# Expert products computed ahead: whole fp32 rows in full-width products, and a later gather in the second layer

## The chip, the cores and the metric

The kernel runs on one core of one Trainium2 chip. The metric is device time in microseconds (us), lower is better. Before the change the median of 3 runs is 5698.48 us (5694.15 to 5700.12).

## The reference

The model is a trunk of two layers over 128 context tokens and 512 latent tokens of width 1024. Each layer has a token mixer (gated linear attention, a short convolution, windowed attention) and then a feed-forward part with 16384 experts, in which each token uses 8 x 16 = 128 of them. The change lies in that second part:

```
q = (xf @ w_pq).reshape(nt, 8, 2, 128)
s = einsum('thpc,hpkc->thpk', q, keys)          # scores against 2 x 128 keys
s1, i1 = top_k(s[:, :, 0], 16);  s2, i2 = top_k(s[:, :, 1], 16)
top_s, top_pos = top_k(s1[..., None] + s2[..., None, :], 16)   # 16 of 256 pairs
eidx = i1 * 128 + i2 at top_pos;  gate = softmax(top_s)
act = gelu(einsum('td,thkd->thk', x, u_tab[eidx]))
out = einsum('thk,thkd->td', gate * act, v_tab[eidx])
```

An expert is a row of `u_tab` and a row of `v_tab`, both of width 1024.

## The kernel before

**Two ways to compute the experts.** For the context tokens and for the first 128 latent tokens of each layer, the rows that a token needs are gathered by indirect DMA (`peer_gather`): per token tile 128 rows of u and 128 rows of v, each fetch 128 x 4 KB, issued by POOL (L915) into one of the slots `grow`. DVE reduces a u row with the token's h (L920), or adds a weighted v row to `gacc` (L932). For the other 384 latent tokens (`TD`) all 16384 experts are computed densely, 128 tiles of 128 experts: S = u tile x h (contraction over 1024 = 8 blocks), GELU, times a gate map G that holds the gate of each (expert, token) and is zero elsewhere, and then the product with the v tile into six accumulators.

**Split products.** A dense product is made of three products: each fp32 operand is split into H (rounded to fp32r, by ACT) and L (the rest, by DVE or POOL), and `mm3` adds H x H, H x L and L x H. For an expert tile `u_hidden` loads 512 KB (`uraw`), ACT makes `uH` (L1012), DVE makes `uL` (L1014), and TensorE runs 8 x 3 products with 384 columns (L196 to L198). hH and hL of the tokens are there already.

**Stages of a layer's second half.** (1) Scores: `routing_keys`, after the mixer. In the first layer the second layer's context pass is run here too. (2) `routing_pairs` for the four token tiles (DVE: top 16 of the pairs); in the first layer this is done in stage 1, in the second one here. (3) Gate maps: `gate_map` for token tiles 1 to 3, each 4 chunks of 4 steps. In a step DVE, POOL and ACT build one-hot rows `oa` and `ob` of 8 tokens, TensorE multiplies them (two groups of 4, `pa` and `po`), and ACT and DVE copy the results into `stage`; after 4 steps the 2 MB of `stage` (one buffer) are stored to `gdr` in DRAM. (4) The dense stage `peer_dense`, 64 pairs of expert tiles.

**Work computed ahead.** In stages 1 to 3, `u_ahead` computes S for the first `AHEAD` = (108, 64) expert tiles, copies it from its bank (tag `po`, two banks, shared with the `po` group of a gate step) to `ust` and stores it to `sdr`. The dense stage takes first the pairs that were not computed ahead (u product, then v product: part one, 32 pairs in the second layer) and then those that were (it loads S from `sdr`, only the v product: part two, 32 pairs).

**What sets the order.** `u_ahead` and `peer_gather` are background generators. `tick` (L152) advances each by its rate for every step of the foreground work: `RU` is the rate of the tiles ahead, `RG` = (2.0, 1.056) that of the gather in stages 2 and 3; in the dense stage the gather's rate is set so that its remaining steps spread evenly over it (`e[1]`, L1396). The scheduler then puts each engine's instructions into one fixed order, in which the engine runs them. A tile's slots are reused in turn: `uraw` has `ucfg["n"]` slots (2 in the gate maps), and the load of the next but one tile waits until a slot's last reader is done.

Of the kernel before, what the change touches and what calls it, by code (L numbers as in the profile page):

```python
# [43 lines left out]
def kernel(ctx: ExitStack, tc: tile.TileContext, A: dict, O: list):  # L44
# [23 lines left out]
    def po2(shape, name="po"):  # L68
        return psum.tile(shape, F32, tag="po", name=name, bufs=2)
# [937 lines left out]
    def u_hidden(l, e, hH, hL):  # L1007

        raw = ucfg["p"].tile([128, 8, 128], F32, name="uraw", bufs=ucfg["n"])
        nc.sync.dma_start(raw.rearrange("p k c -> p (k c)"), A["u_T"][l, e])  # L1010
        uH, uL = t4k([128, 8, 128], "uH", F32R), t4k([128, 8, 128], "uL", F32R)
        act(uH, raw, AF.Copy)  # L1012
        m = 8 - ucfg["pool_l"]
        V.tensor_sub(uL[:, :m, :], raw[:, :m, :], uH[:, :m, :].bitcast(F32))  # L1014
        if m < 8:
            nc.gpsimd.tensor_sub(uL[:, m:, :], raw[:, m:, :], uH[:, m:, :].bitcast(F32))
        ahead = e < AHEAD[l]
        S = po2([128, TD]) if ahead else pb([128, TD])
        if not ahead:
            tick()  # L1020
        for k in range(8):
            mm3(S, uH[:, k, :], uL[:, k, :], hH[:, k, 128:], hL[:, k, 128:], k == 0, k == 7)
        return S

    def u_ahead(l, hH, hL):

# [10 lines left out]
    def peer_dense(s, l, hH, hL, dp, e_g, gout, gp):  # L1037
# [40 lines left out]
                    then(t)  # L1078

        for n, i in enumerate(pairs):  # L1080
            up(i)
            if n and n < 63:
                down()
                down()
# [171 lines left out]
    PIN = (1, 0, 1)  # L1256
    PU = (0, 0, 0, 3)
    OB = ('APDAPADA', 'APDAPADA')
    RG = (2.0, 1.056)
    RU = ((0.7, 1.0), (0.84, 0.8))  # L1260

    CONV = (1, 0.12, (0, 2), (4.8, 4.0), 0.7, 0.2)
# [69 lines left out]
    for l in range(DEPTH):  # L1332
        with pool("g_ctx") as gp:
            gcfg.update(p=gp, tag="grow", n=5, m=0)
            with w_pool(2, 2, PL[1]):
                if l:
                    lat.open_cv()
                    run(lat.finish(l))
                    e = bg_add(peer_gather(C, l, 0, ro_c[0], ro_c[1], gp, after=lat.end), RATE[l][0], PR[2])
                    mixer_lat(l, e, range(4))  # L1340
                else:
                    first = First(gp)
                    e = bg_add(first.work(), RATE[0][0], PR[2])
                    mixer_lat(l, e, range(CONV[0], 4), first)
            bg_drain(e)
        if l + 1 == DEPTH:
            with pool("ln_out") as lp:
                run(ln_finish(C, 2 * DEPTH, ln_rows(lp, 4)))
            nc.gpsimd.dma_start(y_prompt[0], C.x[0])
        with pool("e_lat") as ep:  # L1350
            hH, hL = lat.h
            vals, idxs = route_bufs(Lt, ep)
            ro = {}
            more = l + 1 < DEPTH

            def front(qp):
                yield from routing_keys(Lt, l, hH, hL, vals, idxs, qp)
                if more:
                    for t in range(4):
                        yield from routing_pairs(t, vals, idxs, ep, qp, ro)  # L1360

            ahead = pool("u_t6")
            ucfg.update(p=ahead.__enter__(), n=1, pool_l=PU[0])
            eu = bg_add(u_ahead(l, hH, hL), RU[l][0], PR[0])
            with w_pool(3, 2, PL[2]), pool("ro_lat", 2) as qp:
                with pool("ln_lat2") as lp:
                    run(ln_finish(Lt, 2 * l + 1, ln_rows(lp, 4), True))
                e = bg_add(front(qp), BG[4], PR[5])
                if more:
                    ro_c = ctx_front(l + 1, ec)  # L1370
                bg_drain(e)
            ahead.__exit__(None, None, None)
            gout = []
            ucfg["l"] = l
            with pool("g_lat") as gp, pool("u_lat") as up_:
                ucfg.update(p=up_, n=2, pool_l=PU[1 + l])
                with pool("gm") as qp:
                    gcfg.update(p=qp, tag="grow", n=5, m=1)

                    def pairs(t):  # L1380
                        if not more:
                            for _ in routing_pairs(t, vals, idxs, ep, qp, ro):
                                tick()
                    eu[1] = RU[l][1]
                    pairs(0)
                    e = bg_add(peer_gather(Lt, l, 0, ro[0][0], ro[0][1], gp, gout), RG[l], PR[1])
                    pairs(1)
                    for t in range(1, 4):
                        if t < 3:
                            pairs(t + 1)  # L1390
                        gate_map(t, ro[t], qp)
                    bg_drain(eu)
                ucfg["pool_l"] = PU[3]
                with pool("dense") as dp, w_pool(8, 3, PL[3 + l]):
                    gcfg.update(p=wcfg["p"], tag="wraw", n=8, m=2)
                    e[1] = (256 + LAG - e[3]) / (256 - AHEAD[l] - 10)  # L1396
                    peer_dense(Lt, l, hH, hL, dp, e, gout, gp)


# [109 lines left out]
```

## Time and profile before

| | |
|---|---|
| median of 3 runs (range) | 5698.48 us (5694.15 to 5700.12) |
| the profiled execution: its own time / span of the profile | 5700.02 / 5698.2 us |
| TensorE busy / DVE / ACT / POOL | 90% / 75% / 36% / 44% |
| first layer, gate maps | 2141 to 2505 us |
| second layer, routing pairs and 24 tiles ahead | 4370 to 4506 us |
| second layer, gate maps and 40 tiles ahead | 4506 to 4835 us |
| second layer, dense stage, part one / part two | 4867 to 5356 / 5356 to 5660 us |

The shares over the whole span mix stages with different limits, so the stages of the table are read one by one. A matmul's busy time in the rows is longer than the time for which it holds the array: successive matmuls overlap, so the price of one is the distance between the starts of two. TensorE's granted clock is a mean over a stretch; at each moment it is at one of two levels, 2.4 or 1.2 GHz (1.0 and 0.5).

### The profile page before, as it was taken

How to read it: one execution, taken by the hardware profiler on the slowest of the kernel's cores; microseconds unless marked ns; L12 is line 12 of the kernel's file. 1: busy time of each engine (PE TensorE's matmuls, PEld its weight loads, DVE VectorE, ACT ScalarE, POOL GpSimd, SP SyncE). 2: the span in 40 equal slices, each digit the busy share in tenths (PEclk: the TensorE clock that was granted, in tenths of full speed). 3: DMA queues.
4: the chain of work that ended last, by engine and by line, in shares of the span. 5: the costliest groups of instructions: out<-in, count | busy, mean ns of one | idle time of the engine just before them, and what ended most of it. 6: DMA issues, size and time to landing. Idle time of an engine off the chain costs nothing. (4 is left out here: it accounts for less than half of the span.)

```text
span 5698.2 us, 78492 instructions
## 1 busy us (share of the span) xinstructions
PE 5144.1 (90%) x28598; PEld 4475.9 (79%) x28598; DVE 4257.4 (75%) x7555; ACT 2052.4 (36%) x3456; POOL 2493.1 (44%) x1907
## 2 busy tenths in 40 slices
PE   8998899888899998899999788999989788899997
PEld 6887778767788998888777677777778788799876
DVE  3328878878554868887777798888879998677667
ACT  2214434221232226653333344332223457333332
POOL 1112434676210007876555533456750466444332
PEclk9999999999899999999999899999989899999999
DMA  7762457887666667899999533678842776888895
GB/s 293 269 240 94 156 176 231 297 293 259 212 213 237 226 229 269 307 338 323 325 309 325 186 132 123 225 258 294 293 158 101 233 266 246 310 273 271 285 320 198
DMA packets 456708, 1395.09 MB, mean 245 GB/s; under 512 B 42880, under 2 KB 184832, under 8 KB 413312
## 3 DMA queue, kind: packets, MB, share of 16 engines
q1 hardware_dynamic: 303248, 833.73, 41.3%
q0 software_dynamic: 153072, 556.34, 28.7%
q8 instruction: 225, 3.69, 0.3%
q14 instruction: 163, 1.34, 0.1%
HBM read 1275.29 MB, written 114.62 MB: 244 GB/s over the span
## 5 line engine op out<-in xcount | busy, mean ns | idle before, releaser
L915 POOL DMA_INDIRECT grow<-in_peer_u_dram,eidx x512 | 689.1, 1346 | 675.8 <-DVE gjunk L920 235.8
L915 POOL DMA_INDIRECT grow<-in_peer_v_dram,eidx x512 | 669.3, 1307 | 630.2 <-DVE gacc L932 282.5
L932 DVE SCALAR_TENSOR_TENSOR gacc<-grow,gw,gacc 128x1024 f32<-128x1024 f32 x508 | 707.1, 1392 | 94.8 <-DMA grow<-in_peer_v_dram,eidx 89.8
L176 POOL TENSOR_TENSOR wl<-wraw,wh 128x640 fp32r<-128x640 f32 (+1 forms) x260 | 417.0, 1606 | 703.0 <-ACT wh L172 646.9
L920 DVE SCALAR_TENSOR_TENSOR gjunk<-grow,gh 128x1024 bf16<-128x1024 f32 x512 | 678.1, 1324 | 60.8 <-DMA grow<-in_peer_u_dram,eidx 56.6
L172 ACT ACTIVATE wh<-wraw 128x1024 fp32r<-128x1024 f32 (+1 forms) x388 | 515.2, 1342 | 522.8 <-PE pa L197 207.4
L174 DVE TENSOR_TENSOR wl<-wraw,wh 128x1408 fp32r<-128x1408 f32 (+2 forms) x388 | 555.5, 1434 | 177.2 <-ACT wh L172 177.0
L196 PE MATMUL acc<-wh,daH 128*128 128x512 f32 x1536 | 610.9, 398 | 60.3 <-ACT daH L110 43.8
L198 PE MATMUL acc<-wh,daL 128*128 128x512 f32 x1536 | 612.7, 399 | 14.6 <-DVE daL L111 14.3
L197 PE MATMUL acc<-wl,daH 128*128 128x512 f32 x1536 | 608.4, 396 | 0.5 <-DVE wl L174 0.5
L196 PE MATMUL pa<-hH,wh 128*128 128x512 f32 x1312 | 544.0, 415 | 48.0 <-DVE th L742 12.3
L198 PE MATMUL pa<-hH,wl 128*128 128x512 f32 x1312 | 536.5, 410 | 7.2 <-DVE wl L174 7.2
L197 PE MATMUL pa<-hL,wh 128*128 128x512 f32 x1312 | 536.8, 409 | 0.5 <-DVE hL L111 0.4
L196 PE MATMUL po<-hH,uH 128*128 128x384 f32 x1376 | 490.5, 356 | 26.6 <-ACT uH L1012 10.6
L198 PE MATMUL po<-hH,uL 128*128 128x384 f32 x1376 | 476.6, 347 | 18.4 <-DVE uL L1014 18.1
L197 PE MATMUL po<-hL,uH 128*128 128x384 f32 x1376 | 474.5, 345 | 0.0
L1012 ACT ACTIVATE uH<-uraw 128x1024 fp32r<-128x1024 f32 x256 | 270.8, 1058 | 563.3 <-PE po L197 192.7
L196 PEld LDWEIGHTS acc<-wh,daH 128*128 128x128 f32 x1536 | 294.2, 192 | 130.6 <-ACT daH L110 55.3
L1014 DVE TENSOR_TENSOR uL<-uraw,uH 128x1024 fp32r<-128x1024 f32 (+1 forms) x256 | 285.4, 1115 | 120.0 <-ACT uH L1012 120.0
L985 POOL TENSOR_SCALAR ob<-iota,tt,tt 128x128 f32<-128x128 f32 x192 | 299.3, 1564 | 172.6 <-ACT tt L966 91.8
L198 PEld LDWEIGHTS acc<-wh,daL 128*128 128x128 f32 x1536 | 294.2, 192 | 94.3 <-DVE daL L111 33.4
L196 PEld LDWEIGHTS pa<-hH,wh 128*128 128x128 f32 x1312 | 255.3, 195 | 115.6 <-DVE th L742 14.3
(365 smaller groups left out, 11788.5 us busy)
## 6 DMA issues: line engine op xcount, KB each, us to landing
wraw<-in_w_in_dram SPq DMA_DIRECT2D x168, 1024.0 KB, 5.7
uraw<-in_u_T_dram SPq DMA_DIRECT2D x256, 512.0 KB, 4.7
wraw<-in_v_n_dram SPq DMA_DIRECT2D x256, 512.0 KB, 6.1
wraw<-in_w_mod_dram SPq DMA_DIRECT2D x48, 1024.0 KB, 6.0
wraw<-in_w_branch_dram SPq DMA_DIRECT2D x48, 1024.0 KB, 5.6
gdr<-stage SPq DMA_DIRECT2D x24, 2048.0 KB, 10.4
G<-gdr SPq DMA_DIRECT2D x64, 768.0 KB, 8.0
sdr<-ust SPq DMA_DIRECT2D x172, 192.0 KB, 4.4
```

What stands on the lines that cost most here:

```text
L172: act(H, raw, AF.Copy)
L174: V.tensor_sub(L[:, :m], raw[:, :m], H[:, :m].bitcast(F32))
L176: nc.gpsimd.tensor_sub(L[:, m:], raw[:, m:], H[:, m:].bitcast(F32))
L196: nc.tensor.matmul(out, aH, bH, start=start, stop=False)
L197: nc.tensor.matmul(out, aH, bL, start=False, stop=False)
L198: nc.tensor.matmul(out, aL, bH, start=False, stop=stop)
L915: nc.gpsimd.indirect_dma_start(out=g, out_offset=None, in_=A[tab + str(l)], in_offset=bass.IndirectOffsetOnAxis(ap=eidx[:, j:j + 1], axis=0))
L920: pin(V.scalar_tensor_tensor(junk, g, 1.0, h, op0=OP.mult, op1=OP.mult, accum_out=w[:, j:j + 1]))
L932: pin(V.scalar_tensor_tensor(acc, g, w[:, j:j + 1], acc, op0=OP.mult, op1=OP.add))
L985: (nc.gpsimd if w == "P" else V).tensor_scalar(ob[:, k, :], iota128, TT[1][:, j:j + 1], TT[2][:, j:j + 1], op0=OP.is_equal, op1=OP.mult)
L1012: act(uH, raw, AF.Copy)
L1014: V.tensor_sub(uL[:, :m, :], raw[:, :m, :], uH[:, :m, :].bitcast(F32))
```

## The change

For some of the tiles ahead, TensorE multiplies the loaded rows as they are. `whole_h` adds hH and hL back together into `hF` (one DVE addition of 128 x 3072), and `u_hidden` then does 8 full fp32 products `uraw` x `hF` and no split. This holds for the tiles in the gate maps of the first layer (48 of 108) and for all 64 of the second layer; there `whole_h` runs twice, once in each pool. The dense stage's own tiles stay split. In the second layer the gather's rate in stages 2 and 3 falls from 1.056 to 0.4, and in the dense stage it is 1.35 in part one and what is left, spread evenly, in part two. Counted in the program order on DVE, the 256 gathered rows of the second layer stand as follows: before its first dense pair 83 before and 32 now (20 and 30 of them ahead of the first gate step), in part one 119 and 168, in part two 54 and 56.

```diff
--- before.py
+++ after.py
@@ -1008,6 +1008,12 @@
 
         raw = ucfg["p"].tile([128, 8, 128], F32, name="uraw", bufs=ucfg["n"])
         nc.sync.dma_start(raw.rearrange("p k c -> p (k c)"), A["u_T"][l, e])
+        hF = ucfg.get("hF")
+        if hF is not None:
+            S = po2([128, TD])
+            for k in range(8):
+                nc.tensor.matmul(S, raw[:, k, :], hF[:, k, :], start=k == 0, stop=k == 7)
+            return S
         uH, uL = t4k([128, 8, 128], "uH", F32R), t4k([128, 8, 128], "uL", F32R)
         act(uH, raw, AF.Copy)
         m = 8 - ucfg["pool_l"]
@@ -1021,6 +1027,12 @@
         for k in range(8):
             mm3(S, uH[:, k, :], uL[:, k, :], hH[:, k, 128:], hL[:, k, 128:], k == 0, k == 7)
         return S
+
+    def whole_h(hH, hL, p):
+
+        hF = p.tile([128, 8, TD], F32, name="hF", bufs=1)
+        V.tensor_add(hF, hH[:, :, 128:].bitcast(F32), hL[:, :, 128:].bitcast(F32))
+        return hF
 
     def u_ahead(l, hH, hL):
 
@@ -1078,6 +1090,8 @@
                     then(t)
 
         for n, i in enumerate(pairs):
+            if not i and RD[l]:
+                e_g[1] = (256 + LAG - e_g[3]) / (AHEAD[l] - 10)
             up(i)
             if n and n < 63:
                 down()
@@ -1256,7 +1270,8 @@
     PIN = (1, 0, 1)
     PU = (0, 0, 0, 3)
     OB = ('APDAPADA', 'APDAPADA')
-    RG = (2.0, 1.056)
+    RG = (2.0, 0.4)
+    RD = (None, 1.35)
     RU = ((0.7, 1.0), (0.84, 0.8))
 
     CONV = (1, 0.12, (0, 2), (4.8, 4.0), 0.7, 0.2)
@@ -1360,7 +1375,8 @@
                         yield from routing_pairs(t, vals, idxs, ep, qp, ro)
 
             ahead = pool("u_t6")
-            ucfg.update(p=ahead.__enter__(), n=1, pool_l=PU[0])
+            up_ = ahead.__enter__()
+            ucfg.update(p=up_, n=1 if more else 2, pool_l=PU[0], hF=None if more else whole_h(hH, hL, up_))
             eu = bg_add(u_ahead(l, hH, hL), RU[l][0], PR[0])
             with w_pool(3, 2, PL[2]), pool("ro_lat", 2) as qp:
                 with pool("ln_lat2") as lp:
@@ -1376,6 +1392,7 @@
                 ucfg.update(p=up_, n=2, pool_l=PU[1 + l])
                 with pool("gm") as qp:
                     gcfg.update(p=qp, tag="grow", n=5, m=1)
+                    ucfg["hF"] = whole_h(hH, hL, qp)
 
                     def pairs(t):
                         if not more:
@@ -1390,10 +1407,10 @@
                             pairs(t + 1)
                         gate_map(t, ro[t], qp)
                     bg_drain(eu)
-                ucfg["pool_l"] = PU[3]
+                ucfg.update(pool_l=PU[3], hF=None)
                 with pool("dense") as dp, w_pool(8, 3, PL[3 + l]):
                     gcfg.update(p=wcfg["p"], tag="wraw", n=8, m=2)
-                    e[1] = (256 + LAG - e[3]) / (256 - AHEAD[l] - 10)
+                    e[1] = RD[l] or (256 + LAG - e[3]) / (256 - AHEAD[l] - 10)
                     peer_dense(Lt, l, hH, hL, dp, e, gout, gp)
 
 
```

TensorE in the second layer's gate maps, before: two gate steps and the first three of 24 products of one tile between them (`uH`, `uL` are the halves of the u tile, `oa`, `ob` the one-hot rows).

```order
L993 MATMUL pa<-oa,ob 128x128 x4
L993 MATMUL po<-oa,ob 128x128 x4
L196 MATMUL po<-hH,uH 128x384
L197 MATMUL po<-hL,uH 128x384
L198 MATMUL po<-hH,uL 128x384
...
L993 MATMUL pa<-oa,ob 128x128 x4
L993 MATMUL po<-oa,ob 128x128 x4
```

The same place in the changed kernel.

```order
L993 MATMUL pa<-oa,ob 128x128 x4
L993 MATMUL po<-oa,ob 128x128 x4
L993 MATMUL pa<-oa,ob 128x128
L1015 MATMUL po<-hF,uraw 128x384 x8
L993 MATMUL pa<-oa,ob 128x128 x3
L993 MATMUL po<-oa,ob 128x128 x4
L1015 MATMUL po<-hF,uraw 128x384 x8
```

The tiles stand between the same steps as before; a tile is 8 products in place of 24.

DVE in the same stage, before (`gjunk` is a gathered u row, `ust` the copy of S).

```order
L1014 TENSOR_TENSOR uL<-uraw,uH 128x1024
L980 TENSOR_TENSOR oa<-iota_87,tt_37444 128x1024
L985 TENSOR_SCALAR ob<-iota_87,tt_37448,tt_37452 128x128 x2
L920 SCALAR_TENSOR_TENSOR gjunk,gw<-grow,gh 128x1024
L1031 COPY ust<-po 128x384
L1014 TENSOR_TENSOR uL<-uraw,uH 128x1024
L997 COPY stage<-po 128x4x128
```

And changed.

```order
L997 COPY stage<-po 128x4x128
L980 TENSOR_TENSOR oa<-iota_87,tt_35518 128x1024
L985 TENSOR_SCALAR ob<-iota_87,tt_35522,tt_35526 128x128 x2
L1043 COPY ust<-po 128x384
L997 COPY stage<-po 128x4x128
```

The split and the gathered row are gone from between the gate step's own instructions.

The DMA queue of SP around one store of `stage` in the second layer, before, with the semaphores that each issue waits for.

```order
L1001 DMA gdr<-stage 128x4096 [waits DMAHW3_49,DVE_49,Activation_49]
L1034 DMA sdr_125<-ust 128x384 [waits DMAHW4_49,Activation_49]
L1010 DMA uraw<-in_u_T_dram 128x1024 [waits DMAHW7_49,DMAHW5_49,DVE_49]
L1010 DMA uraw<-in_u_T_dram 128x1024 [waits DMAHW2_49,DVE_49]
L1034 DMA sdr_125<-ust 128x384 [waits DVE_49]
L1010 DMA uraw<-in_u_T_dram 128x1024 [waits DMAHW5_49,DMAHW0_49,DVE_49]
```

And changed.

```order
L1001 DMA gdr<-stage 128x4096 [waits DMAHW2_49,DVE_49,Activation_49]
L1046 DMA sdr_125<-ust 128x384 [waits DMAHW3_49,Activation_49]
L1010 DMA uraw<-in_u_T_dram 128x1024 [waits DMAHW6_49,DMAHW4_49,PE_49]
L1010 DMA uraw<-in_u_T_dram 128x1024 [waits DMAHW0_49,PE_49]
L1046 DMA sdr_125<-ust 128x384 [waits DVE_49]
L1010 DMA uraw<-in_u_T_dram 128x1024 [waits DMAHW7_49,DMAHW4_49,PE_49]
```

A load of a u tile waited for DVE's split of the tile that held the slot; it now waits for TensorE's last product of that tile.

## Rows read from the trace of the kernel before

**Rows 1.** Stretches by stage: per engine busy us and instructions, granted clock, DMA.

```profile
core 0: us, PE busy (x) PEld busy (x) DVE busy (x) ACT busy (x) POOL busy (x), PEclk, DMA share, GB/s
2141.00:2505.00 364.00, 322.64 (x1960) 315.58 (x1959) 316.72 (x442) 242.05 (x514) 296.93 (x189) 0.93 0.81 297
4370.00:4506.00 136.00, 111.89 (x576) 108.03 (x575) 133.75 (x390) 36.70 (x52) 32.29 (x29) 0.89 0.70 228
4506.00:4835.00 329.00, 280.65 (x1729) 273.97 (x1730) 291.72 (x469) 221.78 (x482) 214.53 (x150) 0.91 0.72 254
4867.00:5356.00 489.00, 486.52 (x2452) 442.88 (x2453) 360.97 (x363) 173.92 (x216) 230.23 (x177) 0.99 0.84 283
5356.00:5660.00 304.00, 286.98 (x1224) 231.27 (x1222) 212.01 (x223) 115.58 (x134) 79.71 (x55) 0.97 0.85 292
```

**Rows 2.** Timeline of TensorE, split products of 384 columns: start, duration, instruction.

```profile
4836.18 0.33 PE L196 MATMUL pb<-hH,uH 128*128 128x384 f32 x1
4836.35 0.33 PE L197 MATMUL pb<-hL,uH 128*128 128x384 f32 x1
4836.53 0.33 PE L198 MATMUL pb<-hH,uL 128*128 128x384 f32 x1
```

**Rows 3.** Timeline of TensorE, whole fp32 products of 256, 128 and 512 columns.

```profile
1805.47 3.62 PE L194 MATMUL pa<-wraw,hF 128*128 128x256 f32 x16
1808.92 3.62 PE L363 MATMUL pa<-hF,wraw 128*128 128x128 f32 x31
...
3541.97 1.88 PE L636 MATMUL pb<-rx,perm 128*128 128x512 f32 x4
```

**Rows 4.** Groups by line, TensorE, 2141 to 2505: busy, mean ns, idle, releasers.

```profile
L196 PE MATMUL po<-hH,uH 128*128 128x384 f32 x402 | 145.2, 361 | 0.6 <-ACT uH L1012 0.6
...
L993 PE MATMUL po<-oa,ob 128*128 128x128 f32 x376 | 57.8, 300 | 28.4 <-ACT ust L1033 17.5 <-POOL ob L985 9.4 <-DVE stage L997 1.4
L993 PE MATMUL pa<-oa,ob 128*128 128x128 f32 x376 | 55.3, 287 | 9.9 <-DVE ob L985 4.6 <-DVE oa L980 4.5 <-POOL ob L985 0.6
```

**Rows 5.** Groups by line, TensorE, 4506 to 4835.

```profile
L196 PE MATMUL po<-hH,uH 128*128 128x384 f32 x320 | 114.8, 359 | 5.6 <-DVE stage L997 3.8 <-ACT ust L1033 1.3 <-ACT uH L1012 0.4
...
L993 PE MATMUL po<-oa,ob 128*128 128x128 f32 x368 | 55.8, 297 | 10.5 <-DVE stage L997 9.0 <-POOL ob L985 1.0 <-ACT ust L1033 0.5
L993 PE MATMUL pa<-oa,ob 128*128 128x128 f32 x368 | 54.9, 294 | 28.9 <-ACT stage L999 13.5 <-DVE oa L980 12.6 <-ACT ob L989 2.8
```

**Rows 6.** Groups by line, DVE, 4340 to 4870.

```profile
L1014 DVE TENSOR_TENSOR uL<-uraw,uH 128x1024 fp32r<-128x1024 f32 (+1 forms) x68 | 82.0, 1206 | 5.7 <-ACT uH L1012 5.6
L920 DVE SCALAR_TENSOR_TENSOR gjunk<-grow,gh 128x1024 bf16<-128x1024 f32 x53 | 65.7, 1240 | 23.9 <-DMA grow<-in_peer_u_dram,eidx 23.8
...
L932 DVE SCALAR_TENSOR_TENSOR gacc<-grow,gw,gacc 128x1024 f32<-128x1024 f32 x31 | 40.1, 1293 | 0.1
```

**Rows 7.** Groups by line, ACT, 4340 to 4870.

```profile
L1012 ACT ACTIVATE uH<-uraw 128x1024 fp32r<-128x1024 f32 x69 | 72.9, 1058 | 141.7 <-PE po L197 85.4 <-DMA uraw<-in_u_T_dram 27.5 <-DVE pos L781 10.0
```

**Rows 8.** One tile's instructions (the gather's slot), DVE: ns min/median/max.

```profile
L904 DVE TENSOR_TENSOR gh<-gh,grow x4: 1211/1226/1234, 521.2 to 4396.3; 128x1024 f32<-128x1024 f32 x4
```

**Rows 9.** DMA issues, 2141 to 2510: count, KB each, median us to landing.

```profile
uraw<-in_u_T_dram SPq DMA_DIRECT2D x50, 512.0 KB, 5.5
gdr<-stage SPq DMA_DIRECT2D x11, 2048.0 KB, 11.1
```

**Rows 10.** Waits, 2130 to 2515: us in total, times, longest.

```profile
ACT stage L999 <- DMA gdr<-stage: 26.3, 9, 4.5
...
PE po L993 <- ACT ust L1033: 17.5, 6, 3.8
```

**Rows 11.** Stretches as in rows 1: first layer's dense stage, parts one and two.

```profile
2526.00:2675.00 149.00, 146.33 (x732) 132.44 (x731) 116.78 (x115) 53.43 (x66) 99.27 (x81) 0.99 0.94 339
2700.00:3160.00 460.00, 421.30 (x1743) 333.50 (x1741) 340.41 (x356) 170.46 (x196) 235.01 (x205) 0.96 0.92 319
```

**Rows 12.** The page's costliest groups: the gather's issues on POOL.

```profile
L915 POOL DMA_INDIRECT grow<-in_peer_v_dram,eidx x512 | 669.3, 1307 | 630.2 <-DVE gacc L932 282.5
```

## The prediction

> **What bounds the kernel now.** Read the table by stages first [rows 1]. In the gate maps of the first layer TensorE is busy 323 of 364 us at a granted clock of 0.93, but DVE is busy 317 and POOL 297: no engine is free enough to wait for. In the second layer's routing pairs DVE is busy 134 of 136, so DVE bounds them. In its gate maps DVE has 292 of 329, TensorE 281 at 0.91. In part one of its dense stage TensorE has 486.5 of 489 at 0.99: it alone bounds. Part two is busy 94% and keeps its order here. Then read what ends TensorE's idle time: the releasers in the gate maps are copies and one-hot rows of ACT, DVE and POOL [rows 4, 5], and behind these stands the store of `stage`, for which ACT waits 26 us in the first layer alone [rows 10]. So before, TensorE waits for the others; the question is what its own work becomes.
>
> **The price of a tile.** Split products of 384 columns start 0.35/2 = 0.175 us apart [rows 2]; 24 of them are 4.20 us. A whole fp32 product appears as two records. For 256 columns 16 records take 3.45 us from start to start of the next group, 0.216 each; for 128 columns 31 take 3.62 with a last one of 0.29 (the mean of such a record in rows 4), 0.111 each [rows 3]. That is 0.105 for every 128 columns, so 0.32 at 384; the 512 row bears it out, (1.88 - 0.57)/3 = 0.44 against 0.43 by the step, its tail continued from 0.29 and 0.38 (3.62 - 15 x 0.216). A tile is then 8 x 2 x 0.32 = 5.12 us, 0.92 more than before. On 112 tiles this adds 103 us to TensorE, 44 of it in the first layer, 59 in the second.
>
> In return each tile takes 1.06 us from ACT [rows 7] and 1.21 from DVE [rows 6], 48 tiles and 64.
>
> A rule of the Trainium skill prices it higher: true FP32 takes four passes through the array (FP8 and Floating Point Precision, "TensorE Precision Notes"). Four passes at the split product's 0.175 would be 0.70 per block where the rows give 0.64; its result is among the rivals.
>
> **First layer, gate maps (364 us now).** TensorE's own work: 3 x 402 x 0.175 = 211, and 752 records x 0.111 = 83 [rows 4], 294 together; busy time times clock, 323 x 0.93 = 300, agrees. Idle are 41 us. With the 48 whole tiles the work is 294 + 44 = 338. DVE falls to 317 - 58 = 259, ACT to 242 - 51 = 191, so TensorE is now the longest. What it loses beside: (a) clock, a mean of its two levels of 2.4 and 1.2 GHz. It fell to 0.91 to 0.93 where TensorE sat idle 11 to 15%, and stood at 0.97 in part two of the dense stage with 6% idle [rows 1]; I take 0.97. (b) The u loads. In the changed order a slot is free when TensorE has finished its tile, not when DVE has split it, so no split tile is in reserve: the next but one tile's load begins then and has one tile and a gate step or two (5.1 + 1.8 to 3.6) to land. A load lands in 5.5 us, so it is in time; behind a 2 MB store, which lands in 11.1 [rows 9], it is about even: the store is issued some 1.5 us after the step that fills `stage` (a copy and its issue), lands at 12.6, and the tile is wanted at 2 x 5.12 + 2 x 1.8 = 13.8, while a quarter of the store's time for the load behind it (512 of 2048 KB, 2.8) would end at 15.4 at the latest. That is 0 to 1.6 late; I take 1, for each of 12 stores 12 us. 338/0.97 + 12 = 360: -4. From below, no loss at all: 338, -26. From above, the old idle time and clock: 338/0.93 + 41 = 404, +40. `whole_h` adds 3 x 1.22 = 3.7 us to DVE (three times a 128 x 1024 addition [rows 8]), which here has room.
>
> **Second layer, routing pairs (136 us now).** 24 tiles: 24 x 4.20 = 101 becomes 123. DVE loses 24 x 1.21 = 29, and gains 10 gathered rows that come earlier (30 for 20, 1.24 each, 12) and `whole_h` (3.7): 134 - 13 = 121. Both near 122; 123/0.97 + 3 = 130: -6. Bounds: 123 with nothing lost (-13); the old idle 24 and clock, 123/0.89 + 24 = 162 (+26).
>
> **Second layer, gate maps (329 us now).** Work 960 x 0.175 + 736 x 0.111 = 250 [rows 5] and 5 of the dense stage's first tiles, 255 (281 x 0.91 = 256). 40 whole tiles make it 292. DVE loses 40 x 1.21 and 61 gathered rows at 1.24 to 1.29, about 125: 167 left; ACT loses 42, POOL the fetches. Only TensorE and the store of `stage` are left to bound. 292/0.97 + 12 = 313: -16. Bounds 292 (-37) and 292/0.91 + 48 = 369 (+40). ACT's relief costs nothing to anyone; it is cover that TensorE's longer tile uses up.
>
> **The second `whole_h`** of that layer stands right after the mixer's last hL, ahead of the split of the weights that the scores wait for: 3.7 us on the path, 0 if TensorE has other work: +3.7.
>
> **Dense stage, part one (489 us now).** 49 more rows. DVE 361 + 49 x 1.27 = 423; POOL 230 + 49 x 1.31 = 294 [rows 12]; both have room beside TensorE. DMA: 49 x 0.524 MB (128 rows of 4 KB) over 489 us adds 53 to 283 GB/s, 336. The first layer's part one ran at 339 GB/s, share 0.94, and TensorE was still busy 146.3 of 149, 98.2% against 99.5% here [rows 11]: 1.3% of 489, +6. Bounds: 0; and if it settled at the 91.6% of the first layer's part two (which runs at 319 GB/s), 489 x 99.5/91.6 = 531, +42. Queued behind a late fetch are the slots it shares with the v tiles, and behind these TensorE. Part two keeps its rows (54 and 56): 0.
>
> **Sum.** -4 - 6 - 16 + 3.7 + 6 = -16. The profiled execution took 5700.0, 1.5 above the median of 5698.5: 5684, or 5682 by the median; I say 5683.
>
> **Rivals.**
> 1. The loads are late, so the time is longer. Place: the gate maps of both layers. Price: a slot's load starts only when TensorE leaves it, and if it lands 3 us late at each of 24 stores rather than 1, that is 48 us, and with more idle time the clock would be 0.95 rather than 0.97, (338 + 292)(1/0.95 - 1/0.97) = 14: -16 + 62 = +46, 5744. At 1.3 us late per store and 0.965 it already is a wash. For it: the two slots, the shared `po` banks, ACT's waits for the store [rows 10]. Against it: TensorE's step is longer, which gives a load more time. What the skill says of equal bubbles speaks for looking here: the same gap repeating on the engine that should be saturated can mean too few buffers (Perfetto Trace Analysis, "Optimization Strategy"); the trace of before has no such gap at u loads, since its releasers are copies and one-hot rows [rows 4, 5].
> 2. TensorE stays dense. With DVE and ACT so far below it, it loses 2% and no wait: 338/0.98 = 345 (-19), 123/0.98 = 126 (-10), 292/0.98 = 298 (-31), +3.7, 0: -56, 5642. For it: part one, where the others have room, runs at 99.5%. Against it: the store of `stage` with its one buffer stays.
> 3. The moved rows come back. Part one ends up halfway between its two bounds, +21 rather than +6: -1, 5697. For it: a DMA share near 0.98 by the sum (0.84 x 336/283 = 0.997 by the share of now). Against it: the first layer's part one.
> 4. Four passes. 8 x 4 x 0.175 = 5.60, 0.48 more per tile; 112 x 0.48/0.97 = 55: -16 + 55 = +39, 5737, as a price of one fp32 product of 384 columns of 0.35 per record. For it: nothing in rows 3; against it: both widths beside 384. By that rule of the Trainium skill (FP8 and Floating Point Precision, "TensorE Precision Notes") the change would be slower; no row of before shows 384 whole columns.
>
> **How the numbers follow.** Forecast 0.39 (its own range 5668 to 5701), rival 1 0.24, rival 2 0.19, rival 3 0.12, rival 4 0.06. A measurement of this kernel tells 0.2% (11 us) from no change, so faster means below 5687 and slower above 5710. Faster: the forecast 0.24, rival 2 0.19, of rival 3 0.01: 0.44. Same: the forecast 0.13, rival 1 0.03, rival 3 0.08: 0.24. Slower: the forecast 0.02, rival 1 0.21, rival 3 0.03, rival 4 0.06: 0.32. The range for 8 in 10 runs from rival 2 to nearly rival 1, with the ends of the bounds left out: 5638 to 5738.
>
> **What the changed profile would show.** The price: records of `po<-hF,uraw` 0.32 us apart, 1792 of them, and no `uH` or `uL` before the dense stage of the second layer. The gate maps: TensorE's clock at 0.96 or more and DVE under 75% in the first layer, under 60% in the second; if TensorE's idle time there is mostly ended by the DMA of `uraw`, rival 1 holds. The first gate step of the second layer comes about 3 us earlier from the scores' start (-6 + 3.7). Part one: TensorE busy over 98% at some 335 GB/s; under 96%, and rival 3 holds. The forecast is wrong if the records are further apart than 0.33, or if the first layer's gate maps take over 375 us.

## The result

The changed kernel takes 5779.6 us (median of 4 runs, 5773.43 to 5786.9) against 5699.3 before (4 runs, 5694.15 to 5706.98): ratio 1.014, 95% interval [1.0123, 1.0158]. It is slower by 80 us; 5683 was forecast, with a range to 5738. The profiled execution took 5786.9 us (span 5785.1).

The time is best split at events that both traces have. "Gate maps" runs here from TensorE's last score product to DVE's first `da` of the dense stage. The changes below add up to 87 us, not 80, because the profiled execution of the changed kernel stands 7 us above its median. Each stage's time comes from one trace. The first stretch, which has the same work in all fourteen kernels of this case, took between 2120 and 2131 us, so a few us in a stage are not told from nothing.

| us | before | after | change | forecast |
|---|---|---|---|---|
| start to last score product, first layer | 2123.5 | 2129.3 | +6 | 0 |
| first layer, gate maps | 402.3 | 471.1 | +69 | -4 |
| first layer, dense stage, and mixer to the last hL | 1727.0 | 1746.2 | +19 | 0 |
| second layer, scores (last hL to last product) | 107.1 | 115.0 | +8 | +3.7 |
| second layer, pairs (to the first gate step) | 146.6 | 156.0 | +9 | -6 |
| second layer, gate maps | 358.9 | 343.4 | -15 | -16 |
| dense stage, part one / part two | 504.4 / 328.4 | 509.9 / 314.2 | +5 / -14 | +6 / 0 |

The same stretches as in [rows 1], then the two halves of the first layer's gate maps (columns as there):

```profile
core 0: us, PE busy (x) PEld busy (x) DVE busy (x) ACT busy (x) POOL busy (x), PEclk, DMA share, GB/s
2166.00:2566.00 400.00, 347.67 (x1487) 238.72 (x1488) 253.71 (x380) 190.09 (x459) 240.81 (x192) 0.93 0.74 267
4475.00:4617.00 142.00, 129.31 (x388) 73.97 (x386) 132.47 (x412) 11.49 (x22) 32.70 (x32) 0.98 0.69 233
4617.00:4930.00 313.00, 302.75 (x1404) 213.82 (x1404) 162.56 (x304) 181.45 (x445) 116.44 (x96) 0.98 0.49 170
4961.00:5471.00 510.00, 504.01 (x2534) 459.13 (x2535) 428.72 (x441) 180.67 (x223) 315.73 (x228) 0.99 0.93 328
...
2201.50:2436.50 235.00, 187.84 (x770) 125.93 (x769) 172.84 (x252) 97.26 (x235) 164.69 (x132) 0.91 0.87 317
2464.00:2580.00 116.00, 113.72 (x516) 78.96 (x515) 46.04 (x73) 62.42 (x147) 40.39 (x32) 0.99 0.50 175
```

The first layer's gate maps have two faces. In the first half TensorE is busy 0.80 of the time and DVE 0.74 (busy over length); in the second TensorE is at 0.98 and DVE at 0.40. A mean over both hides this: it shows three engines far from full. The cause is in DVE's fixed order. Gathered rows between one group of four gate steps and the next, counted in that order:

```
before   6  9  8  8  7  9  8  8  7  9  8 10
after    7 14 16 15 16 15 12  0  0  0  0  2
```

The gather is issued at the same rate of 2.0 per step. With the splits gone, the scheduler placed the rows on DVE about twice as densely, until none were left. (With the additions of `whole_h` but the splits kept, in experiment 7, 7 to 10 rows stand in each group.) One instance, DVE's timeline (start, duration, instruction, idle time before it and what ended it):

```profile
2239.84 1.32 DVE L920 SCALAR_TENSOR_TENSOR gjunk<-grow,gh 128x1024 bf16<-128x1024 f32 x1 [0.97 <-DMA grow<-in_peer_u_dram,eidx]
...
2242.32 1.29 DVE L920 SCALAR_TENSOR_TENSOR gjunk<-grow,gh 128x1024 bf16<-128x1024 f32 x1 [1.16 <-DMA grow<-in_peer_u_dram,eidx]
...
2247.19 1.23 DVE L920 SCALAR_TENSOR_TENSOR gjunk<-grow,gh 128x1024 bf16<-128x1024 f32 x1 [3.57 <-DMA grow<-in_peer_u_dram,eidx]
...
2248.34 0.55 DVE L1043 COPY ust<-po 128x384 f32<-128x384 f32 x1
```

and TensorE's at the same place:

```profile
2234.25 5.33 PE L1015 MATMUL po<-hF,uraw 128*128 128x384 f32 x16
2239.41 1.05 PE L993 MATMUL pa<-oa,ob 128*128 128x128 f32 x8
2240.30 1.06 PE L993 MATMUL po<-oa,ob 128*128 128x128 f32 x8
2248.95 7.28 PE L1015 MATMUL po<-hF,uraw 128*128 128x384 f32 x16 [7.59 <-DVE ust L1043]
```

The copy of the finished tile needs 0.55 us, but stands behind three rows whose fetches are not there; TensorE waits 7.59 us for the bank. The first line also gives the price: 16 records in 2239.41 - 2234.25 = 5.16 us, 0.323 each. Summed over the first half, waits (us in total, times, longest):

```profile
PE po L1015 <- DVE ust L1043: 32.9, 10, 7.6
ACT stage L999 <- DMA gdr<-stage: 28.7, 6, 5.4
DVE gjunk L920 <- DMA grow<-in_peer_u_dram,eidx: 28.7, 16, 5.8
POOL grow L915 <- DVE gjunk L920: 20.2, 11, 5.1
DVE gacc L932 <- DMA grow<-in_peer_v_dram,eidx: 18.0, 8, 4.8
```

It is a ring: DVE waits for a fetch, POOL waits to issue the next until DVE has freed a slot. Before, between 2200 and 2430 us, DVE waited for v rows not at all and for u rows this long:

```profile
DVE gjunk L920 <- DMA grow<-in_peer_u_dram,eidx: 5.3, 2, 3.6
```

TensorE's idle time over the whole stage, the answer to [rows 4]:

```profile
L1015 PE MATMUL po<-hF,uraw 128*128 128x384 f32 x725 | 259.7, 514 | 37.0 <-DVE ust L1043 35.8 <-DMA uraw<-in_u_T_dram 1.2
L993 PE MATMUL po<-oa,ob 128*128 128x128 f32 x368 | 51.6, 284 | 15.1 <-DVE stage L997 10.4 <-POOL ob L985 4.6
```

Late u loads, the first rival, are 1.2 us of it. That is not because they land sooner where the time is lost: between 2200 and 2430 us they land in 7.1 us and the stores in 13.0 (medians; before 5.1 and 10.9). In the second layer the additions show. The timeline of the scores:

```profile
4345.26 3.27 DVE L111 TENSOR_TENSOR hL<-lnrow,hH 128x512 fp32r<-128x512 f32 x2 [0.60 <-ACT hH L110]
...
4348.57 4.59 DVE L1034 TENSOR_TENSOR hF<-hH,hL 128x3072 f32<-128x3072 f32 x1
...
4353.09 5.56 DVE L174 TENSOR_TENSOR wl<-wraw,wh 128x1408 fp32r<-128x1408 f32 x2
...
4355.82 0.29 PEld L198 LDWEIGHTS pa<-hH,wl 128*128 128x128 f32 x1 [6.81 <-DVE wl L174]
...
4473.45 10.99 PE L1015 MATMUL po<-hF,uraw 128*128 128x384 f32 x26 [11.57 <-DVE hF L1034]
```

Before, the split `wl` was done ahead of the last hL and nobody waited for it; now it stands behind the addition, and TensorE waits 6.8 us. The second addition stands behind the pairs' first rounds on DVE, and TensorE waits 11.6 us for it. In the pairs TensorE waits almost as long for u loads, 11.1 us:

```profile
L1015 PE MATMUL po<-hF,uraw 128*128 128x384 f32 x384 | 129.8, 499 | 23.7 <-DVE hF L1034 11.6 <-DMA uraw<-in_u_T_dram 11.1 <-DVE top L780 1.1
```

and in the second layer's gate maps not at all:

```profile
L1015 PE MATMUL po<-hF,uraw 128*128 128x384 f32 x640 | 214.8, 490 | 2.4 <-DVE stage L997 1.9 <-DVE ust L1043 0.5
L993 PE MATMUL pa<-oa,ob 128*128 128x128 f32 x368 | 52.0, 286 | 3.8 <-DVE oa L980 1.9 <-ACT stage L999 1.8
L993 PE MATMUL po<-oa,ob 128*128 128x128 f32 x368 | 51.2, 282 | 3.3 <-POOL ob L985 3.2
```

### The profile page after: what moved, and what is told of

It is laid out like the page before. It is cut to its first block, busy times and chain, and to the rows that moved or that the text cites. A ratio compares the mean times of both kernels' runs of the same rounds, so it can differ in the third digit from the quotient of the medians.

```text
span 5785.1 us, 76442 instructions
## 1 busy us (share of the span) xinstructions
PE 5236.6 (91%) x27702; PEld 4329.7 (75%) x27702; DVE 4156.5 (72%) x7446; ACT 1943.1 (34%) x3342; POOL 2425.7 (42%) x1907
## 5 line engine op out<-in xcount | busy, mean ns | idle before, releaser
L1015 PE MATMUL po<-hF,uraw 128*128 128x384 f32 x1792 | 618.5, 502 | 63.2 <-DVE ust L1043 36.3
L1015 PEld LDWEIGHTS po<-hF,uraw 128*128 128x128 f32 x1792 | 343.8, 196 | 293.8 <-DVE ust L1043 38.8
L985 POOL TENSOR_SCALAR ob<-iota,tt,tt 128x128 f32<-128x128 f32 x192 | 242.5, 1270 | 435.5 <-issue 158.9
L197 PEld LDWEIGHTS acc<-wl,daH 128*128 128x128 f32 x1536 | 293.2, 191 | 60.3 <-DVE wl L174 1.0
L363 PE MATMUL pa<-hF,wraw 128*128 128x128 f32 x2560 | 321.8, 280 | 7.3 <-DVE hF L313 2.8
L363 PEld LDWEIGHTS pa<-hF,wraw 128*128 128x128 f32 x2560 | 305.7, 194 | 18.4 <-issue 5.5
```

The costliest lines, as they stand in the source:

```text
L197: nc.tensor.matmul(out, aH, bL, start=False, stop=False)
L363: nc.tensor.matmul(q[:, f, :], WH[:, k, f * 128:(f + 1) * 128], hH[:, k, :], start=k == 0, stop=k == 7)
L985: (nc.gpsimd if w == "P" else V).tensor_scalar(ob[:, k, :], iota128, TT[1][:, j:j + 1], TT[2][:, j:j + 1], op0=OP.is_equal, op1=OP.mult)
L1015: nc.tensor.matmul(S, raw[:, k, :], hF[:, k, :], start=k == 0, stop=k == 7)
```

## The experiments

Ratios are to the kernel before, with 95% intervals; the kernel before ran at 5694 to 5706 us beside them. VectorE, ScalarE and GpSimd in the expectations are DVE, ACT and POOL.

**1. The rows kept in their places.** The rows of the gate maps keep their place in program order; nothing else changes. Rows per four steps: 4 8 8 8 7 8 9 8 7 8 9 14.

```diff
-    PIN = (1, 0, 1)
+    PIN = (1, 1, 1)
```

> The changed kernel, with DVE's uses of the gathered rows kept in the order in which the program issues them while the gate maps run (8 rows per 4 gate steps in the first layer, as before the change, where the changed kernel has 14 to 16 in the first 28 steps and none in the last 20). Theory A (the scheduler bunched the rows; DVE waits for their fetches and holds back the copies that free TensorE's banks): the first layer's gate maps fall from 434 us (first gate step to first dense pair) to about 385, the whole to about 5735. Rival B (a whole tile's longer time on TensorE is the loss): under 10 us gained, 5770 to 5780. The second layer has a few rows more among its gate steps: 0 to +5 by both.

Measured 5723.7, 1.0045 [1.0031, 1.0058]. The first layer's gate maps fall from 471 to 431 us; counted from the first gate step, as the expectation does, from 434 to 394, where theory A had 385. Rival B is out. The stretch from its first gate step:

```profile
2168.00:2545.00 377.00, 354.12 (x1572) 245.95 (x1571) 258.46 (x382) 192.58 (x466) 252.11 (x192) 0.96 0.83 292
```

```profile
L1015 PE MATMUL po<-hF,uraw 128*128 128x384 f32 x768 | 263.4, 497 | 6.2 <-ACT ob L989 2.8 <-ACT ust L1045 1.3 <-ACT ob L988 0.9
```

TensorE's idle time before tiles falls from 37.0 to 6.2 us with the same DVE work (258 against 254): the order cost it, not the work. The whole edit is worth 1.014 - 1.0045, some 54 us. The profiles put 40 of them in this stage and 5 in the second layer's pairs, where the edit leaves 7 rows ahead of the first gate step in place of 30. Another 7 lie in the first layer's dense stage and mixer, which the edit does not touch.

**2. The change in the second layer alone.**

```diff
-                    ucfg["hF"] = whole_h(hH, hL, qp)
+                    ucfg["hF"] = None if more else whole_h(hH, hL, qp)
```

> The changed kernel with the first layer's gate maps split as before; whole rows and the later gather in the second layer only. Both theories: the first layer's 25 + 49 us up to the first dense pair come back (8 of them were there before any changed instruction), about -66: 5713. What is left against before is the second layer alone: by its trace -7 (+11 and +6 before the gate steps, -15 in them, +5 and -14 in the dense stage), so 5692; if the 12 us in the first layer's dense stage and 5 in the second mixer belong to the change, about 5712.

Measured 5700.11, 1.0003 [0.9989, 1.0017]. The first layer's gate maps are back at 399. So whole rows there cost the whole loss, 78 us by the ratios (66 were expected); the second layer's half is worth nothing in sum, with an interval of -6 to +10 us. Experiments 3 and 4 take that nothing apart.

**3. Whole rows alone**, the gather where it was.

```diff
-    RG = (2.0, 0.4)
-    RD = (None, 1.35)
+    RG = (2.0, 1.056)
+    RD = (None, None)
```

> Whole rows in both layers, the second layer's gather at its old rates. If the gather's move is what pays in the second layer, its gate maps bunch too (6, 7, 7 and then 21 rows in 4 steps stand in the order), DVE waits there as in the first layer, and the time is 20 to 40 us above the changed kernel: 5800 to 5820. If the move is worth nothing (theory C: it comes back in the dense stage), 5770 to 5780.

Measured 5798.89, 1.0174 [1.0152, 1.0195], 19 us over the changed kernel by the ratios, just under what was expected if the move pays (the two intervals just overlap). The second layer's gate maps do bunch: 1, 6, 7, 7 and 21 rows stand in its first groups of four steps, then next to none, and its pairs and gate maps together take 512 us against the changed kernel's 499.

**4. The gather's move alone**, all tiles split: the kernel before with the two `RG`, `RD` lines of the change and what reads them.

> Before, with only the later gather in the second layer (rates 0.4, then 1.35 and the rest), all products split. DVE loses some 60 rows of 1.27 us in gate maps where it is busy 292 of 329 us, about 75 us, of which TensorE can use what it sat idle for (48) and the clock: -15 to -30 there; part one of the dense stage +5 by the changed kernel's trace: 5675 to 5690. Theory C: no change, 5695 to 5705.

Measured 5643.0, 0.9895 [0.9877, 0.9912]: faster than both kernels, and by more than was expected (5675 at the least). The second layer's pairs, gate maps and part one:

```profile
4380.00:4484.00 104.00, 98.07 (x547) 95.65 (x547) 101.87 (x279) 32.84 (x48) 18.18 (x15) 0.98 0.72 238
4484.00:4800.00 316.00, 281.17 (x1788) 274.49 (x1786) 263.63 (x487) 230.65 (x502) 142.54 (x116) 0.95 0.55 196
4819.00:5326.00 507.00, 501.90 (x2533) 457.14 (x2534) 428.90 (x443) 180.68 (x224) 314.02 (x228) 0.99 0.94 332
```

The pairs fall from [rows 1]'s 136 us to 104, near TensorE's own price of 24 split tiles (101). DVE has 32 us less to do there. Some 12 of them are rows, of which only 10 stand ahead of the first gate step; some 13 are selection work of the pairs themselves, which the new order puts behind that step (16 reductions to `sel`, L847, stand ahead of it in place of 20). The border between the two stages has moved, so they are best taken together: 505 us before, 455 here. Part one takes the 49 rows for some 2 us. Rows alone (+99 us by the ratio) and move alone (-60) make +39, measured is +80. A reading that fits: the move frees an engine, DVE, that whole rows had freed already, and whole rows load the engine, TensorE, that bounds once DVE is free. With the move in place whole rows cost the second layer 1.0003 - 0.9895, 62 us; 64 x 0.92 is 59, but the 62 also hold the additions, which experiment 7 prices.

**5. Eight slots for gathered rows** beside the gate maps, the order still bunched.

```diff
-                    gcfg.update(p=qp, tag="grow", n=5, m=1)
+                    gcfg.update(p=qp, tag="grow", n=8, m=1)
```

> The changed kernel with eight slots for gathered rows beside the gate maps instead of five; the order of the rows on VectorE stays bunched (14 to 16 per four gate steps in the first layer). Theory A1 (in the bunched stretch VectorE waits for the fetch of a row, 31.7 + 18.0 us, because only five fetches can be under way, and TensorE waits behind it for its PSUM copies): the first layer's gate maps, 434 us in the changed kernel from its first gate pair to its first dense pair, fall to 395 to 405, the whole to 5740 to 5750. Theory A2 (the bunched rows cost by VectorE's own time, 1.23 to 1.29 us each, not by the fetch): the gate maps stay at 425 to 434 and the whole within 10 us of 5780. Rival B (the price of a tile, and not the bunching): no change, within 5 us of 5780.

Measured 5764.56, 1.0115 [1.009, 1.0141]: between the two theories. Gate maps 455. Waits of the bunched half:

```profile
ACT stage L999 <- DMA gdr<-stage: 25.6, 6, 4.8
...
PE po L1015 <- DVE ust L1043: 20.5, 8, 8.9
...
DVE gjunk L920 <- DMA grow<-in_peer_u_dram,eidx: 12.2, 5, 4.4
DVE stage L997 <- DMA gdr<-stage: 11.3, 4, 3.4
```

DVE's wait for u rows falls from 28.7 to 12.2 us, but now it waits 11.3 for the store of `stage`, and TensorE waits 9.2 for u loads, where it had waited 1.2.

**6. All copies of tiles on ScalarE.**

```diff
-            if e % 2:
-                V.tensor_copy(st, S)
-            else:
-                act(st, S, AF.Copy)
+            act(st, S, AF.Copy)
```

> The changed kernel with every copy of a tile's product out of PSUM (ust) on ScalarE; before, every second one was VectorE's. The bunched order of the rows stays. Theory A (VectorE stands at a row whose fetch is not there, the copy behind it is late, and TensorE waits for the bank: 37.0 us on ust by VectorE, 15.1 on stage): the first layer's gate maps fall from 434 us by 20 to 35, the whole to 5745 to 5760; the wait on stage stays. Rival (TensorE has no work because the transfers are late, whoever copies): gate maps 430 to 440, the whole within 8 us of 5780. Against it: ScalarE has 190 of 400 us busy there and would be at some 230, so it can itself become late in the second layer's pairs, plus 5 at most.

Measured 5770.9, 1.0123 [1.0099, 1.0148]: gate maps 464, 7 less instead of 20 to 35, a miss. The groups of TensorE in the bunched half say why:

```profile
L1015 PE MATMUL po<-hF,uraw 128*128 128x384 f32 x390 | 139.8, 514 | 3.9 <-DMA uraw<-in_u_T_dram 2.0 <-ACT ust L1042 1.8
L993 PE MATMUL po<-oa,ob 128*128 128x128 f32 x200 | 32.0, 310 | 41.2 <-DVE stage L997 34.9 <-POOL ob L985 6.3
```

The 32.9 us on `ust` went to the copy that DVE kept, `stage`: 34.9. Who holds the bank changes with the edit; that DVE stands at a fetch does not.

**7. The additions alone**: experiment 4, and `whole_h` called in the three places with nothing reading its sum.

```diff
+            if not more:
+                whole_h(hH, hL, ap_)
...
+                    whole_h(hH, hL, qp)
```

> The gather's move alone (5643.0), with the addition of the two halves of h (whole_h) also made where the changed kernel makes it: in the second layer's scores and at the head of both gate stages. Nothing reads the sum; all tile products stay split. Theory C (in the second layer most of the 57 us that whole rows cost is the place of the two additions on VectorE and what waits behind them): 5655 to 5670, with the second layer's last scores to its first tile at 133 to 136 us. Rival D (it is the price of the tiles, 0.92 us each, and their place in the order): 5643 to 5650, scores 123 to 127 us.

Measured 5668.23, 0.9949 [0.9935, 0.9964], as theory C had it in total: 31 us over experiment 4 by the ratios. In the profiles: first layer's gate maps +8 (407 against 399; the kernel before had 402), second layer's scores +8, its pairs and gate maps +5. TensorE's wait for `wl` is there again, 6.8 us. So C is right that the additions cost several times their 3.4 us each, and wrong that they are most of the second layer's loss: some 14 of 62.

**8. Two `stage` buffers**, on experiment 4.

```diff
-            stage = qp.tile([128, 128, 32], F32, name="stage", bufs=1)
+            stage = qp.tile([128, 128, 32], F32, name="stage", bufs=2)
```

> The gather's move alone (5643.0) with two buffers for a gate step's staged rows (stage) instead of one. Theory E (in the gate maps the copy into stage waits for the store of the step before: 26.3 us of ScalarE's waits in the second layer before, and TensorE waits for the copy): each layer's gate maps fall by 5 to 15 us, the whole to 5620 to 5635. Rival F (TensorE is the bound there, 0.93 and more of the stretch, the wait is covered): 5638 to 5648. Rival G (the stores now collide with the loads of tiles, and the copies come late): 5650 to 5665.

Measured 5619.05, 0.9857 [0.9839, 0.9874], the fastest version. The second layer's gate maps:

```profile
4472.00:4776.00 304.00, 275.72 (x1782) 269.97 (x1782) 261.00 (x482) 229.03 (x499) 135.71 (x115) 0.96 0.56 204
```

12 us less than in experiment 4; the first layer's gate maps gain nothing (404 against 399), so theory E holds in one of its two places. (The 26.3 us that it names are those of the first layer [rows 10]; in the second ACT waited 17.9.) The rest of the 24 us lies in other stages, 11 of it in the first layer's dense stage and mixer, and the profiles don't settle why.

**9. No u loads** in the first layer's gate maps of the changed kernel: one tile is loaded, and its product is repeated.

```diff
+        one = ucfg.get("one") if hF is not None else None
+        if one is None:
+            raw = ucfg["p"].tile([128, 8, 128], F32, name="uraw", bufs=ucfg["n"])
...
+        else:
+            raw = one
```

> The changed kernel, with the loads of the u tiles left out in the first layer's gate maps: one tile is loaded and all 48 products there use it, so their values are not the reference's. The rows stay bunched on VectorE (14 to 16 per four gate steps), TensorE's and VectorE's work is the same. Theory A3 (in the bunched stretch the transfers are at their limit: 13 MB per four steps, of which 2 MB are u tiles, at 317 GB/s; so the rows come late whatever waits for them): a store of stage comes every 34 us there instead of 39, last keys to first dense pair falls from 471 us to 435 to 445, the whole to 5740 to 5755. Theory A1 (too few slots: a fetch takes so long from issue to landing that five cannot keep up, and the rate is not at its limit): 460 to 471, the whole 5770 to 5780. Eight slots gave 455 with 338 GB/s in that stretch and more waits on u loads, which speaks for both.

Measured 5755.45, 1.0096 [1.0079, 1.0113]. The total lies where A3 had it, the stage does not: gate maps 465, where A1 had 460 to 471, and a store of `stage` about every 40 us, as in the changed kernel. The bunched half, and DVE's waits in it:

```profile
2197.00:2427.00 230.00, 179.84 (x758) 121.01 (x759) 172.89 (x254) 95.95 (x231) 173.81 (x131) 0.93 0.75 269
...
DVE gjunk L920 <- DMA grow<-in_peer_u_dram,eidx: 28.4, 15, 6.0
...
DVE gacc L932 <- DMA grow<-in_peer_v_dram,eidx: 20.8, 10, 6.0
```

With 269 GB/s in place of 317 DVE waits for rows as long as in the changed kernel (28.7 and 18.0), so A3 falls. Too few slots, A1, is left as a part of the cause: experiment 5 gave 16 us. What makes up the rest of the lateness stays open; two `stage` buffers with the bunched order were not run. Most of the fall in the total is outside the stage (dense stage 643 against 661), where nothing was changed; its cause stays open.

**10. Rows in their places and two buffers**, on the changed kernel (the edits of 1 and 8).

> The changed kernel with the rows of the gate maps kept in their places (as in the run at 5723.7) and with two stage buffers. Theory P (once the rows are spread and the gather is moved, TensorE bounds both gate stages, so that whole rows cost their price, 112 x 0.92 = 103 us, less what stays hidden, whatever else is mended): 5619 plus 70 to 100 = 5690 to 5720, TensorE busy over 95% in both gate maps. Rival (whole rows pay once VectorE, ScalarE and the stores no longer wait for each other): at or under 5619.

Measured 5717.51, 1.0027 [1.0016, 1.0038]. The first layer's gate maps from the first gate step, then pairs and gate maps of the second layer:

```profile
2164.00:2540.00 376.00, 351.88 (x1560) 243.38 (x1559) 258.04 (x379) 195.67 (x467) 251.57 (x192) 0.96 0.80 290
4428.00:4560.00 132.00, 120.54 (x373) 69.84 (x372) 128.61 (x424) 9.90 (x23) 13.71 (x14) 0.99 0.52 175
4560.00:4875.00 315.00, 305.00 (x1438) 215.28 (x1438) 165.39 (x267) 191.63 (x462) 141.79 (x116) 0.99 0.58 201
```

With both mended, whole rows stand 97 us over experiment 8 (1.0027 - 0.9857), as theory P had the total. Not all of it is the price of the tiles, though. Experiment 7 gives 31 us to the additions, which would leave 66 of the 103; and the pinned order is a second difference between the two kernels, which no run tells apart. The sign that P named, TensorE busy over 95%, came in the second layer (305 of 315 us) and not in the first (352 of 376). In the second layer DVE has 165 of 315 us to do; the trade gave time to an engine that had it.

**11 and 12. The first layer's gather slower or faster** beside its gate maps, on experiment 8: `RG` (1.6, 0.4), then (2.4, 0.4).

> The gather's move alone with two stage buffers (5619.0), and the first layer's gather also slower beside the gate maps (rate 1.6 instead of 2.0; some 16 rows more left to its dense stage). If VectorE still costs TensorE time in the first layer's gate maps (404 us from last keys to first dense pair): 390 to 400 there, the dense stage 0 to 5 longer, the whole 5605 to 5620. If the first layer's dense stage is at the limit of its transfers (319 to 339 GB/s before), the rows cost there what they free: 5617 to 5635.

> The gather's move alone with two stage buffers (5619.0), and the first layer's gather faster beside its gate maps (rate 2.4 instead of 2.0: some 19 rows fewer left to its dense stage). With rate 1.6 the gate maps had become 14 us shorter and the dense stage 39 longer. If a row costs in the dense stage more than beside the gate maps wherever one starts: gate maps 404 plus 10 to 15, dense stage 645 minus 20 to 35, the whole 5600 to 5612. If the rate 2.0 already leaves the dense stage as many rows as it hides: dense stage 640 to 645, gate maps plus 10 to 15, the whole 5625 to 5640.

Measured 5651.86, 0.9911 [0.9895, 0.9928], and 5636.26, 0.9868 [0.9845, 0.9891], the second not told from experiment 8 by its interval. Gate maps 390, 404, 432 and dense stage 684, 645, 627 us at the rates 1.6, 2.0, 2.4: what one stage gains the other more than loses, either way. The first total lies above both of its alternatives. The second lies where its second alternative had it, but by other parts: the gate maps grew by 28 us, not 10 to 15, and the dense stage fell by 18.

## Why the prediction was wrong, step by step

**The price of a tile** was right: 0.323 us per record, 0.32 by the sum from [rows 3]; rival 4, at 0.35, is out. The rule named there is that of four passes (the Trainium skill, FP8 and Floating Point Precision, "TensorE Precision Notes"). The trace agrees with it in what further columns cost: 128 more add 2 x 0.105 = 0.21 us to a whole product [rows 3] and 0.054 to a split one (starts 0.173 us apart at 384 columns and 0.227 at 512, medians of the trace before), 3.9 times as much. What I had wrong was the price of a pass: of the 0.175 from start to start only 3 x 0.054 = 0.16 goes with the columns, and four times 0.16 is the 0.65 us measured.

**First layer, gate maps, "338/0.97 + 12 = 360: -4": the step that failed**, +69. Its total of work was right (354 x 0.96 = 340 us with the rows spread, 338 forecast). I took DVE's relief, 317 to 259 us, as room spread evenly over the stage. The scheduler used it at once: 95 rows in the first seven groups of four steps, 2 in the last five. There DVE's own work is 172.8 of 235 us, and with the fetch waits of 47 it is nearly always taken, in the order that also holds TensorE's copies. Experiment 1 gives 40 of the 69 back. The other 29 are not taken apart by a run of their own. If the 8 us of experiment 7 for the addition at the stage's head hold here too, 21 are left to the tile's price: TensorE has 354 of 377 us to do in experiment 1, so of the 44 us about half was covered, not all. I had written that the forecast fails above 375; the stretch took 400.

**The first and the second rival.** The time came out beyond that of rival 1, but in the gate maps, where it placed the loss, not by its mechanism: u loads ended 1.2 us of TensorE's waits in the first layer's and none in the second's. What ended them was a copy, as in [rows 10], where ACT's copy held TensorE up for 17.5 us already. By the Trainium skill (Perfetto Trace Analysis, "Optimization Strategy") the same gap recurring on the engine that should be full can mean too few buffers. Here it recurs ten times, 32.9 us, and more slots took 12 us of that and 16 of the stage: partly so. Rival 2 had TensorE dense everywhere: 0.97 busy in the second layer's gate maps, 0.91 in its pairs and 0.87 in the first layer's gate maps speak against it.

**Second layer, pairs, -6**: +9. TensorE's 123 was right (experiment 1 has 126.7 busy in them), but I allowed it 3 us of waits and it had 24: 11.6 for the second addition, which I had counted as 3.7 us of DVE's work and no wait, and 11.1 for u loads. There rival 1's mechanism did show, outside the place that it named; with 7 rows ahead of the first gate step in place of 30 (experiments 1 and 10) these loads cost 2.1 and 2.8 us. DVE stayed busy 132 of 142, not 121, since the new order also puts more selection work ahead of that step (24 reductions to `sel` in place of 20).

**Second layer, gate maps, -16**: -15, and 313 us forecast and measured for the stretch. TensorE bounds it as forecast, 303 of 313 us, but so near a number is luck in part: the 12 us for late loads came to nothing, while the work was 303 x 0.98 = 297 in place of 292 and TensorE waited 10 us for copies and one-hot rows. Pairs and gate maps together gave -6, where -22 was forecast. **`whole_h`, +3.7**: +8, since `wl` was queued behind it; I counted the instruction, not what it pushes. **Part one, +6**: +5, with TensorE busy 98.8% at 328 GB/s (98.2% and 336 forecast) and a DMA share of 0.93; the "near 0.98" of rival 3 has no row behind it. **Part two, 0**: -14; experiments 2 and 4, which have the new gather rate, show it (-14, -11) and 3, without it, does not (+3), so it goes with the moved gather.

Not in the sum: +19 us in the first layer's dense stage and mixer, where the changed kernel issues the same work. Experiments with whole rows in the first layer show +1 to +12 there (1, 3, 5, 6, 9, 10), those without -7 to +5 (2, 4, 7, 8), so part of it may belong to them. What makes it stays open.

**The wrong frame** behind it: I credited the second layer's gain to the pair of edits. It is the gather's move alone that pays (-60), and whole rows in the second layer, with their additions, give up all of it (+62).

## What to carry to other kernels

Work taken off an in-order engine leaves a hole that the scheduler may fill with everything it has ready; count the new order in pieces of the stage, not over the whole, and look at what stands behind each wait for a transfer. Do not buy relief for one engine with work on another before asking which of them bounds the stage once each other edit is in: two edits that relieve the same engine do not add. Where copies that free another engine's buffers share a queue with work that waits for far memory, pin the latter's places (40 us of 471 here).

## What the runs showed of the hardware

A whole fp32 product of 384 columns is two records of 0.323 us, 5.16 us for eight, 1.23 times the 24 split products' 4.20. After a wait of 7.59 us the same 16 records took 7.28 us instead of 5.33, so this wait cost TensorE 2 us more than its length: the granted clock was 0.73 while they ran and 1.00 in the tile before the wait. A tile after a wait of 2.00 us took 5.43, at 1.00. Fewer bytes moved (269 in place of 317 GB/s) did not shorten VectorE's waits for gathered rows (49 us in place of 47).
